# Moving every large SBUF tile of a hybrid decoder layer to an address that is a multiple of 256 bytes

## The chip, the cores and the metric

One core of a Trainium2 chip runs the whole program in one launch. The metric is the device time of one execution in microseconds; the median of three runs before the change is 1642.38 us (1641.95 to 1642.83).

## The reference, cut to what matters

One decoder layer on 1024 tokens of width 1024, all in float32. Everything that the change can touch is matrix products and the tiles that feed them:

```
n    = rmsnorm(x)
p    = n @ w_in                     # columns: z 1024 | x 1024 | B 256 | C 256 | dt 16 | q, k, v 1024 each
dt   = softplus(p_dt + dt_bias)     # 16 heads
y_s  = SSD(conv(x, B, C), dt) * silu(z), grouped rmsnorm
y_a  = (softmax(q1 k1) - lambda softmax(q2 k2)) v, 8 heads, causal, rmsnorm
h    = x + concat(y_s, y_a) @ w_out
h    = h + (silu(n2 @ w_gate) * (n2 @ w_up)) @ w_down,   n2 = rmsnorm(h)
out  = rmsnorm(h)
```

## The kernel before

**Products.** Both operands of a large product are split into two float32r parts, high and low (`split`, L170: a cast on ACT, then a subtraction on DVE), and `mm3` (L126) adds three matmuls in PSUM: high by high (L127), high by low (L128), low by high (L129). Each matmul has its own load of 128x128 stationary weights (PEld) and streams the other operand, the moving one: 256 or 512 columns, 264 in the pass that the change rewrites. TensorE therefore sees one weight load for each matmul all through the kernel. Transposes and the attention's `o` product are plain float32.

**Stages, in order of time.** Norm and transpose of the input (to about 48 us), the gate of group 0 with dt (`gate_dt`, two passes of 264 columns, to 75 us), convolutions and SSD scan of both groups with the second gate between them (to about 395 us, mixed with the first attention head's projections), attention (to about 865 us), the output projection (`po_s`, `po_a`, `po_b`, to about 975 us), the FFN's gate and up by seven products (`x`, `y`, `z`, to 1414 us), the down projection in the same way (`dx`, `dy`, `dz`, to the end). Outside the FFN's first part the order on each engine comes from a scheduler that simulates the program when it is built, with due times and priorities; inside `tc.manual_schedule` the order on PE is that of the code.

**SBUF.** Tiles live in pools that are laid out one behind the other; a tag with `bufs=n` owns n slots, each as large as the tag's largest tile. The addresses of this program, in bytes within a partition:

| pool | holds | first address | modulo 256 |
|---|---|---|---|
| const | ident (512), mhalf (32), pcol (276, takes 288) | 16512 | 128 |
| small | columns of 4 to 32 bytes | 17344 | 192 |
| big | nhi, nlo, yh, yl, n2, gd: 4 x 16384 | 18144 | 224 |
| wp | raw 2, wh 3, wl 3 slots of 4224 | 83680 | 224, 96, 224, 96, ... |
| a4, p4, hx, ob, cv | 4096 or 2048 a slot | 117472 and on | 224 throughout |

The slot of 4224 bytes comes from the gate pass: 4 x 264 columns x 4 bytes. It is 16.5 x 256, so neighbouring slots of `wp` differ by 128 modulo 256. `wh` has its slots at 92128, 96352 and 100576 (224, 96, 224 modulo 256), `wl` at 104800, 109024 and 113248 (96, 224, 96); all other large tiles stand at 224. In the FFN one slot holds the high and the low part of one product's weights (stationary), and the products take wh and wl slots in turn; in `proj_nat`, `out_block` and `proj_z0` a wh and a wl slot are the moving operand; in `proj_T` they are stationary; in the down projection both operands are in such slots.

**The gate pass.** `z0_raw` (L180) loads two units of 4 row blocks x 264 columns for each of two passes: pass 0 holds 16 dt columns and 248 gate columns, pass 1 the remaining 264. The raw tag has 2 slots. Pass 0 is loaded between the third and the fourth input block on SP's queue, its splits stand behind the third normalised block, and `proj_z0` (L258) runs 8 blocks of 128 tokens over 8 row blocks, 24 matmuls each, 192 in a pass. Each block's gate columns go through SiLU on ACT (L368) and to DRAM `z_d` from POOL's queue (L370).

Of the kernel before, what the change touches and what calls it, by code (L numbers as in the profile page):

```python
# [9 lines left out]
F32 = mybir.dt.float32  # L10
F32R = mybir.dt.float32r
# [6 lines left out]
P = 128  # L18
# [6 lines left out]
def tile_hybrid_block(  # L25
# [56 lines left out]
    nc.vector.memset(mhalf, -0.5)  # L82
    pcol = const.tile([P, 69], F32, name="pcol")
    CW, CB, SN, SL = 0, 48, 60, 68
# [9 lines left out]
    def norm_rows(parts, wbc, outs, name, pool=(), junk=None):  # L94
        """outs = RMSNorm of the row whose column pieces are parts; pieces in pool are weighted on Pool and scaled on ACT"""
        n, w = len(parts), DM // len(parts)
        ss = small.tile([P, n], F32, tag="ss1", name="ss_" + name)
        for i, p in enumerate(parts):
            nc.scalar.activation(outs[i] if junk is None else junk, p, AF.Square, accum_out=ss[:, i:i + 1])
        if n > 1:  # L100
            s1 = small.tile([P, 1], F32, tag="ss1", name="st_" + name)
            nc.vector.tensor_tensor(s1, ss[:, 0:1], ss[:, 1:2], op=ALU.add)
            ss = s1
        r = rstd_of(ss, DM, name)
        for i, (p, o) in enumerate(zip(parts, outs)):
            wi = wbc[:, i * w:i * w + w]
            if i in pool:
                nc.gpsimd.tensor_tensor(o, p, wi, op=ALU.mult)
                nc.scalar.mul(o, o, r)
            else:  # L110
                nc.vector.scalar_tensor_tensor(o, p, r, wi, op0=ALU.mult, op1=ALU.mult)
# [51 lines left out]

# [1 line left out]
    def load_raw(src, shape, name):  # L165
# [12 lines left out]
    w_in_k = w_in2.rearrange("(k p) c -> p k c", p=P)  # L178

    def z0_raw(a, u):  # L180
        """columns of dt and of the gate of group 0: 264 of 528"""
        raw = wp.tile([P, 4, 264], F32, tag="raw", bufs=2, name=f"wr_z0_{a}_{u}")
        k = slice(4 * u, 4 * u + 4)
        if a == 0:
            nc.sync.dma_start(raw[:, :, 0:16], w_in_k[:, k, C_DT:C_DT + 16])
            nc.sync.dma_start(raw[:, :, 16:264], w_in_k[:, k, C_Z:C_Z + 248])
        else:
            nc.sync.dma_start(raw, w_in_k[:, k, C_Z + 248:C_Z + 512])
        return raw

    def z0_unit(raw, a, u):
        hi = wp.tile([P, 4, 264], F32R, tag="wh", bufs=3, name=f"wh_z0_{a}_{u}")
        lo = wp.tile([P, 4, 264], F32R, tag="wl", bufs=3, name=f"wl_z0_{a}_{u}")
        split(hi, lo, raw)
        return hi, lo

# [1 line left out]
    xs = []  # L198
    mixw = P4([P, DM], F32, "mixw")
    for t in range(NT):  # L200
        xt = A4([P, DM], F32, f"x_{t}")
        nc.sync.dma_start(xt, x2[t * P:(t + 1) * P, :])
        xs.append(xt)
        if t == 0:
            nc.sync.dma_start(mixw, mix_norm_w[0].partition_broadcast(P))
        if t == 2:
            zraw = [z0_raw(0, u) for u in range(2)]
    nhi = [B16([P, KD, 512], f"nhi{i}") for i in range(2)]
    nlo = [B16([P, KD, 512], f"nlo{i}") for i in range(2)]
    for t in range(NT):  # L210
        norm_transpose([xs[t]], mixw, nhi, nlo, t, (CV if t % 2 else P4)([P, DM], F32, f"xm_{t}"), SC, f"n{t}",
                       (0,) if t % 2 else ())
        if t == 2:
            zus = [z0_unit(zraw[u], 0, u) for u in range(2)]

# [1 line left out]
    prow = P4([69, P], F32, "prow")  # L217
# [5 lines left out]
    nc.tensor.transpose(pps, prow, ident[:69, :69])  # L223
    nc.vector.tensor_copy(pcol, pps)
    nc.vector.tensor_scalar(pcol[:, SL:SL + 1], pcol[:, SL:SL + 1], 1.0 - LAMBDA_INIT, None, op0=ALU.mult)
# [9 lines left out]

# [1 line left out]
    def w_unit(src, shape, name, alloc=None):  # L237
# [10 lines left out]
    def proj_T(*jobs):  # L248
        """each job: a weight, a column, a name and sink(half, psum [128 columns, 512 tokens])"""
        us = [w_unit(w_k[:, :, col:col + P], [P, KD, P], name) for w_k, col, name, _ in jobs]  # L250
        for half in range(2):
            for (hi, lo), (_, _, name, sink) in zip(us, jobs):
                ps = MM([P, 512], f"mm_{name}_{half}")
                for k in range(KD):
                    mm3(ps, hi[:, k, :], lo[:, k, :], nhi[half][:, k, :], nlo[half][:, k, :], k == 0, k == KD - 1)
                sink(half, ps)

    def proj_z0(us, name, sink):  # L258
        """units of 264 columns; sink(t, psum [128 tokens, 264])"""
        for t in range(NT):  # L260
            ps = (MS if t % 4 > 1 else MM)([P, 264], f"mm_{name}_{t}")
            tk = slice((t % 4) * P, (t % 4) * P + P)
            for k in range(KD):
                hi, lo = us[k // 4]
                mm3(ps, nhi[t // 4][:, k, tk], nlo[t // 4][:, k, tk], hi[:, k % 4, :], lo[:, k % 4, :],
                    k == 0, k == KD - 1)
            sink(t, ps)

    def proj_nat(col, name, sink):
        """256 columns; sink(t, psum [128 tokens, 2 blocks from t, 256])"""  # L270
        us = [w_unit(w_in_k[:, 4 * u:4 * u + 4, col:col + 256], [P, 4, 256], f"{name}_{u}") for u in range(2)]
# [9 lines left out]

# [1 line left out]
    W16 = [P, NT, 16]  # L283
# [49 lines left out]

# [1 line left out]
    def conv_tiles(*tiles):  # L335
# [21 lines left out]
    def gate_dt():  # L357
        """the gate of group 0 and dt"""
        for a in range(2):
            zt = [None]  # L360
            w0, w = (0, 248) if a == 0 else (248, 264)

            def sink(t, ps):
                if t % 2 == 0:
                    zt[0] = CV([P, 2, w], F32, f"zt0_{a}_{t}")
                if a == 0:
                    nc.vector.tensor_tensor(adt[:, t, :], ps[:, 0:16], hv[:, 0, :], op=ALU.add)
                nc.scalar.activation(zt[0][:, t % 2, :], ps[:, 264 - w:], AF.Silu)  # L368
                if t % 2 == 1:
                    nc.gpsimd.dma_start(z_d[t - 1:t + 1, :, w0:w0 + w].rearrange("t p c -> p t c"), zt[0])  # L370
            proj_z0(zus if a == 0 else [z0_unit(z0_raw(1, u), 1, u) for u in range(2)], f"z0_{a}", sink)

# [138 lines left out]

# [1 line left out]
    cneg = sp.tile([P, P], F32, tag="cs", name="cneg")  # L513
# [13 lines left out]
    def v_pair(hh):  # L527
        # [head][block] views of the two heads; in the last pair but one, the heads' tiles are freed one by one
        by_head = hh == NH // 2 - 2
# [129 lines left out]

# [1 line left out]
    KG = 4  # L661
# [14 lines left out]
    def out_block(t, kys, ws, name, bank=MM):  # L676
        """two token blocks from t, 256 columns"""
        ps = bank([P, 2, 256], f"po_{name}_{t}")
# [47 lines left out]

# [1 line left out]
    # gate and up by Winograd's seven products: A are two column tiles by two halves of the contraction, B the two  # L728
    # halves of the contraction by two halves of the tokens; C = A B is summed up in PSUM (X, Y and Z)
    ORDER = (1, 2, 6, 5, 7, 3, 4)  # L730
# [4 lines left out]
    def room(p, early):  # L735
        """an operand B: [hi or lo][block of 128 rows] views of 512 tokens"""
        if early:
# [59 lines left out]
    def ffn_pair(pr, raws, order=ALL, ybank=SC):  # L797
        """silu(gate) * up of two column tiles; they and their sums as operands of the down projection to g_d"""
        sg, tm, c22, reg, sm = {}, {}, {}, [{}, {}], [{}, {}]
# [145 lines left out]
    def final_half(t, nh, last):  # L945
        """the first half of a row to be ready is weighted before its scale is known"""
        ho = h_parts(ho_all, t)
# [12 lines left out]

    # down, by the same seven products: A are the two halves of the tokens by two row tiles, B the row tiles by two
    # halves of the columns
    SLOT = {2: 0, 4: 1, 1: 2, 7: 3, 5: 4, 6: 5, 3: 6}
# [28 lines left out]
    for gi, prs in enumerate(groups):  # L992
# [5 lines left out]
        def psums(two, name):  # L998
            """four banks: one for each block of 128 tokens of a half"""
            if two:  # L1000
# [81 lines left out]
```

## Time and profile before

| | |
|---|---|
| median of 3 runs | 1642.38 us |
| the profiled execution, first to last instruction | 1643.3 us (no other time of it is recorded; 0.9 us above the median) |
| TensorE clock granted, mean | 0.995 |
| PE, weight loads, DVE, ACT, POOL busy | 97%, 84%, 65%, 47%, 26% of the span |
| DMA | 172.78 MB, mean 105 GB/s |

A matmul's record lasts longer than its share of TensorE, since matmuls overlap: 512 columns have a record of about 0.39 us and the next one starts after about 0.23 us. What a matmul costs is the distance from its start to the start of the next, and that is read from the timeline: the first and the last start of a stretch, divided by the matmuls between them. Where a row of the timeline merges n instructions, their spacing is (length - one record) / (n - 1).

### The profile page before, as it was taken

The numbers are of one execution on the slowest core, as the hardware profiler recorded it, in microseconds if no ns is written. First come the engines' busy times: TensorE is split into PE (matmuls) and PEld (weight loads), VectorE is DVE, ScalarE is ACT, GpSimd is POOL, SyncE is SP. The second block draws the span as 40 slices with busy tenths as digits, with TensorE's granted clock in tenths as the row PEclk, the third lists the DMA queues.
The fourth block names the chain that finished last, engine by engine and source line by source line (L and its number), as shares of the span: only waits on it lengthen the run. The fifth ranks groups of instructions, "written<-read, shape, count | busy, mean of one in ns | idle before, by whom it ended". The sixth has DMA issues, their size and how long they took to land. (4 is left out here: it accounts for less than half of the span.)

```text
span 1643.3 us, 23716 instructions
## 1 busy us (share of the span) xinstructions
PE 1597.2 (97%) x9170; PEld 1386.9 (84%) x9170; DVE 1071.6 (65%) x1682; ACT 775.8 (47%) x1608; POOL 429.2 (26%) x378
## 2 busy tenths in 40 slices
PE   6999999999999999999999998999999999999997
PEld 6988878887989989889999987888888888778885
DVE  5345745688776676677674477455555555898987
ACT  6444764456555565575552245333333333334445
POOL 4100330032000000013300034444444443542322
PEclk9999999999999999999999999999999999999999
DMA  5321451143011110147523221233333323944122
GB/s 195 110 79 52 129 163 56 36 142 92 24 46 39 46 33 27 45 130 229 162 77 116 84 99 56 96 102 104 111 116 118 98 96 134 365 166 186 39 103 103
DMA packets 105291, 172.78 MB, mean 105 GB/s; under 512 B 7813, under 2 KB 75530, under 8 KB 103770
## 3 DMA queue, kind: packets, MB, share of 16 engines
q1 hardware_dynamic: 95210, 137.11, 25.2%
q0 software_dynamic: 9968, 34.15, 6.3%
q8 instruction: 72, 1.18, 0.3%
q14 instruction: 41, 0.34, 0.1%
HBM read 125.82 MB, written 45.42 MB: 104 GB/s over the span
## 5 line engine op out<-in xcount | busy, mean ns | idle before, releaser
L127 PE MATMUL x<-n,wa 128*128 128x512 f32 x352 | 138.7, 396 | 0.0
L128 PE MATMUL x<-n,wa 128*128 128x512 f32 x352 | 138.7, 394 | 0.0
L129 PE MATMUL x<-n,wa 128*128 128x512 f32 x352 | 137.8, 394 | 0.0
L590 ACT ACTIVATE p<-s,nmx 128x256 f32<-128x256 f32 (+7 forms) x128 | 94.4, 740 | 53.2 <-DVE nmx L588 49.9
L172 ACT CAST wa<-s 128x512 fp32r<-128x512 f32 x88 | 54.7, 622 | 132.3 <-PE x L129 59.4
L173 DVE TENSOR_TENSOR wa<-s,wa 128x512 fp32r<-128x512 f32 x88 | 76.8, 873 | 51.1 <-ACT wa L172 50.8
L172 ACT CAST dg<-gd 128x512 fp32r<-128x512 f32 x77 | 47.7, 620 | 114.7 <-PE dx L129 57.2
L588 DVE TENSOR_REDUCE nmx<-s 128x1 f32<-128x256 f32 (+7 forms) x128 | 95.3, 754 | 2.4
L173 DVE TENSOR_TENSOR dg<-gd,dg 128x512 fp32r<-128x512 f32 x77 | 66.2, 862 | 23.3 <-ACT dg L172 23.2
L129 PEld LDWEIGHTS x<-n,wa 128*128 128x128 f32 x352 | 66.5, 189 | 15.1
L128 PEld LDWEIGHTS x<-n,wa 128*128 128x128 f32 x352 | 66.6, 189 | 14.8
L127 PEld LDWEIGHTS x<-n,wa 128*128 128x128 f32 x352 | 66.6, 189 | 14.8
L127 PE MATMUL mm_z<-wh_z,nhi 128*128 128x264 f32 (+1 forms) x256 | 75.9, 298 | 2.3 <-ACT wh_z L172 2.3
L611 PE MATMUL o<-v,p 128*128 128x128 f32 x576 | 77.7, 275 | 0.0
L129 PE MATMUL mm_z<-wh_z,nlo 128*128 128x264 f32 (+1 forms) x256 | 77.3, 303 | 0.0
L611 PEld LDWEIGHTS o<-v,p 128*128 128x128 f32 x576 | 73.5, 191 | 2.7
L128 PE MATMUL mm_z<-wl_z,nhi 128*128 128x264 f32 (+1 forms) x256 | 75.0, 294 | 0.0
L127 PE MATMUL mm_v<-wh_v,nhi 128*128 128x256 f32 x256 | 74.2, 290 | 0.0
L129 PE MATMUL mm_v<-wh_v,nlo 128*128 128x256 f32 x256 | 74.1, 290 | 0.0
L128 PE MATMUL mm_v<-wl_v,nhi 128*128 128x256 f32 x256 | 73.5, 287 | 0.0
L128 PE MATMUL po_a<-wl_wo,yh 128*128 128x256 f32 x256 | 72.6, 283 | 0.0
L91 POOL TENSOR_TENSOR rs_o<-ms_o,mhalf 128x4 f32<-128x4 f32 x16 | 18.0, 1125 | 208.4 <-DVE ms_o L89 208.3
(331 smaller groups left out, 5172.9 us busy)
## 6 DMA issues: line engine op xcount, KB each, us to landing
gd<-g_d SPq DMA_DIRECT2D x11, 1792.0 KB, 7.8
wr_g<-in_w_gate_dram SPq DMA_DIRECT2D x22, 512.0 KB, 3.8
wr_u<-in_w_up_dram SPq DMA_DIRECT2D x22, 512.0 KB, 4.3
g_d<-sg SPq DMA_DIRECT2D x22, 512.0 KB, 5.1
wr_d<-in_w_down_dram SPq DMA_DIRECT2D x22, 512.0 KB, 5.0
L<-cs_d POOLq DMA_DIRECT2D x16, 512.0 KB, 4.4
wr_y<-yT_d SPq DMA_DIRECT2D x16, 512.0 KB, 3.8
wr_wo<-in_w_out_dram SPq DMA_DIRECT2D x16, 512.0 KB, 3.5
```

The source lines that it names most:

```text
L91: nc.gpsimd.tensor_tensor(r, ms, mhalf[:, :w], op=ALU.pow)
L127: nc.tensor.matmul(ps, lh, rh, start=first, stop=False, skip_group_check=more)
L128: nc.tensor.matmul(ps, lh, rl, start=False, stop=False, skip_group_check=more)
L129: nc.tensor.matmul(ps, ll, rh, start=False, stop=last, skip_group_check=more)
L172: nc.scalar.copy(hi, raw)
L173: nc.vector.tensor_tensor(lo, raw, hi.bitcast(F32), op=ALU.subtract)
L588: nc.vector.reduce_max(nmx[:, m:m + 1], s[:, :Lk], axis=AX.X, negate=True)
L590: nc.scalar.activation(p[:, :Lk], s[:, :Lk], AF.Exp, bias=nmx[:, m:m + 1], accum_out=sm[:, m:m + 1])
L611: nc.tensor.matmul(o, wT[:, j * P:(j + 1) * P], vt[h % 2][j], start=(j == 0), stop=(j == i))
```

## The change

`pcol` grows from 69 to 77 columns (276 to 308 bytes; in blocks of 32 that is 288 to 320), which moves everything behind it by 32 bytes, so 18144 becomes 18176 = 71 x 256. The gate pass is cut anew: pass 0 has 272 columns (16 of dt, 256 of the gate) in three units of 3, 3 and 2 row blocks, pass 1 has 256 columns in two units of 4. The largest unit is then 4096 bytes, the eight slots of `wp` take 4096 bytes each, and with that every slot of big, wp, a4, p4, hx, ob and cv stands at a multiple of 256. Comments and docstrings are dropped too. Cut to its core:

```
-    pcol = const.tile([P, 69], F32, name="pcol")
+    pcol = const.tile([P, 77], F32, name="pcol")
...
+    Z0 = ((272, (0, 3, 6, 8)), (256, (0, 4, 8)))
+
     def z0_raw(a, u):
-        raw = wp.tile([P, 4, 264], F32, tag="raw", bufs=2, name=f"wr_z0_{a}_{u}")
-        k = slice(4 * u, 4 * u + 4)
+        w, ks = Z0[a]
+        k = slice(ks[u], ks[u + 1])
+        raw = wp.tile([P, ks[u + 1] - ks[u], w], F32, tag="raw", bufs=2, name=f"wr_z0_{a}_{u}")
         if a == 0:
             nc.sync.dma_start(raw[:, :, 0:16], w_in_k[:, k, C_DT:C_DT + 16])
-            nc.sync.dma_start(raw[:, :, 16:264], w_in_k[:, k, C_Z:C_Z + 248])
-        else:
-            nc.sync.dma_start(raw, w_in_k[:, k, C_Z + 248:C_Z + 512])
+        nc.sync.dma_start(raw[:, :, w - 256:], w_in_k[:, k, C_Z + a * 256:C_Z + a * 256 + 256])
         return raw
 
     def z0_unit(raw, a, u):
-        hi = wp.tile([P, 4, 264], F32R, tag="wh", bufs=3, name=f"wh_z0_{a}_{u}")
-        lo = wp.tile([P, 4, 264], F32R, tag="wl", bufs=3, name=f"wl_z0_{a}_{u}")
+        w, ks = Z0[a]
+        shape = [P, ks[u + 1] - ks[u], w]
+        hi = wp.tile(shape, F32R, tag="wh", bufs=3, name=f"wh_z0_{a}_{u}")
+        lo = wp.tile(shape, F32R, tag="wl", bufs=3, name=f"wl_z0_{a}_{u}")
         split(hi, lo, raw)
-        return hi, lo
+        return [(hi[:, k, :], lo[:, k, :]) for k in range(shape[1])]
...
-            zraw = [z0_raw(0, u) for u in range(2)]
+            zraw = [z0_raw(0, u) for u in range(3)]
...
-            zus = [z0_unit(zraw[u], 0, u) for u in range(2)]
+            zus = [z0_unit(zraw[u], 0, u) for u in range(3)]
...
-    def proj_z0(us, name, sink):
+    def proj_z0(us, w, name, sink):
+        ks = [k for u in us for k in u]
         for t in range(NT):
-            ps = (MS if t % 4 > 1 else MM)([P, 264], f"mm_{name}_{t}")
+            ps = (MS if t % 4 > 1 else MM)([P, w], f"mm_{name}_{t}")
             tk = slice((t % 4) * P, (t % 4) * P + P)
-            for k in range(KD):
-                hi, lo = us[k // 4]
-                mm3(ps, nhi[t // 4][:, k, tk], nlo[t // 4][:, k, tk], hi[:, k % 4, :], lo[:, k % 4, :],
-                    k == 0, k == KD - 1)
+            for k, (hi, lo) in enumerate(ks):
+                mm3(ps, nhi[t // 4][:, k, tk], nlo[t // 4][:, k, tk], hi, lo, k == 0, k == KD - 1)
             sink(t, ps)
...
-            w0, w = (0, 248) if a == 0 else (248, 264)
+            w = Z0[a][0]
...
-                    zt[0] = CV([P, 2, w], F32, f"zt0_{a}_{t}")
+                    zt[0] = CV([P, 2, 256], F32, f"zt0_{a}_{t}")
...
-                nc.scalar.activation(zt[0][:, t % 2, :], ps[:, 264 - w:], AF.Silu)
+                nc.scalar.activation(zt[0][:, t % 2, :], ps[:, w - 256:], AF.Silu)
```

More of the change, by code (lines that the diff above doesn't have):

```diff
@@ L223, in tile_hybrid_block @@
     nc.tensor.transpose(pps, prow, ident[:69, :69])
-    nc.vector.tensor_copy(pcol, pps)
+    nc.vector.tensor_copy(pcol[:, :69], pps)
     nc.vector.tensor_scalar(pcol[:, SL:SL + 1], pcol[:, SL:SL + 1], 1.0 - LAMBDA_INIT, None, op0=ALU.mult)
@@ L360, in gate_dt @@
             zt = [None]
-            w0, w = (0, 248) if a == 0 else (248, 264)
+            w = Z0[a][0]
             def sink(t, ps):
                 if t % 2 == 0:
-                    zt[0] = CV([P, 2, w], F32, f"zt0_{a}_{t}")
+                    zt[0] = CV([P, 2, 256], F32, f"zt0_{a}_{t}")
                 if a == 0:
                     nc.vector.tensor_tensor(adt[:, t, :], ps[:, 0:16], hv[:, 0, :], op=ALU.add)
-                nc.scalar.activation(zt[0][:, t % 2, :], ps[:, 264 - w:], AF.Silu)
+                nc.scalar.activation(zt[0][:, t % 2, :], ps[:, w - 256:], AF.Silu)
                 if t % 2 == 1:
-                    nc.gpsimd.dma_start(z_d[t - 1:t + 1, :, w0:w0 + w].rearrange("t p c -> p t c"), zt[0])
-            proj_z0(zus if a == 0 else [z0_unit(z0_raw(1, u), 1, u) for u in range(2)], f"z0_{a}", sink)
+                    nc.gpsimd.dma_start(z_d[t - 1:t + 1, :, a * 256:a * 256 + 256].rearrange("t p c -> p t c"), zt[0])
+            proj_z0(zus if a == 0 else [z0_unit(z0_raw(1, u), 1, u) for u in range(2)], w, f"z0_{a}", sink)
     def gate(g):
```

## The prediction

> **What bounds the kernel now.** I read the page first, then the busy times of eleven stretches (the table of windows), then single rows of the timeline, since the question is what one matmul costs.
>
> ```profile
> span 1643.3 us, 23716 instructions
> PE 1597.2 (97%) x9170; PEld 1386.9 (84%) x9170; DVE 1071.6 (65%) x1682; ACT 775.8 (47%) x1608; POOL 429.2 (26%) x378
> ```
> ```profile
> core 0: us, PE busy (x) PEld busy (x) DVE busy (x) ACT busy (x) POOL busy (x), PEclk, DMA share, GB/s
> 8.00:75.00 67.00, 59.91 (x450) 58.79 (x451) 32.58 (x62) 36.22 (x60) 20.99 (x19) 0.97 0.42 138
> ...
> 301.50:395.00 93.50, 91.45 (x557) 76.88 (x556) 77.87 (x123) 52.77 (x122) 21.75 (x28) 1.00 0.31 97
> 395.00:718.00 323.00, 323.00 (x2041) 290.03 (x2040) 222.64 (x436) 190.62 (x470) 17.01 (x21) 1.00 0.15 45
> ...
> 1010.00:1414.00 404.00, 404.00 (x1758) 329.92 (x1756) 210.26 (x263) 135.07 (x225) 179.43 (x124) 1.00 0.34 114
> 1414.00:1634.00 220.00, 215.51 (x925) 172.48 (x923) 198.64 (x283) 97.89 (x184) 77.25 (x56) 1.00 0.38 146
> ```
> PE is busy 97% of the span at the full clock (1.00 from 75 us on). In the FFN, 1010 to 1414 us, it never stops: 404.00 us for 1758 matmuls, 229.8 ns each. DMA is at 0.42 of its engines or below in these rows. So time is matmuls times spacing, except in the down projection, where DVE is busy 198.64 of 220.00 us. I take the median as the base; the profiled span is 0.9 us above it.
>
> **What one matmul costs, by address.** These rows are from the timeline, first and last start of a stretch of back-to-back matmuls.
>
> ```profile
> 1201.05 0.39 PE L127 MATMUL y<-n,wa 128*128 128x512 f32 x1
> ...
> 1203.77 0.39 PE L127 MATMUL z<-n,wa 128*128 128x512 f32 x1
> 1204.23 0.40 PE L127 MATMUL x<-n,wa 128*128 128x512 f32 x1
> ...
> 1207.02 0.39 PE L127 MATMUL x<-n,wa 128*128 128x512 f32 x1
> 1502.80 0.39 PE L127 MATMUL dz<-dw,dg 128*128 128x512 f32 x1
> ...
> 1505.13 0.39 PE L129 MATMUL dz<-dw,dg 128*128 128x512 f32 x1
> 929.24 0.28 PE L128 MATMUL po_b<-wl_wo,yh 128*128 128x256 f32 x1
> ...
> 932.00 0.28 PE L127 MATMUL po_b<-wh_wo,yh 128*128 128x256 f32 x1
> 872.47 0.28 PE L127 MATMUL po_a<-wh_wo,yh 128*128 128x256 f32 x1
> ...
> 875.27 0.28 PE L127 MATMUL po_a<-wh_wo,yh 128*128 128x256 f32 x1
> 100.59 0.39 PE L127 MATMUL mm_x<-nhi,wh_x 128*128 128x512 f32 x1
> ...
> 102.67 0.39 PE L127 MATMUL mm_x<-nhi,wh_x 128*128 128x512 f32 x1
> 41.87 0.28 PE L127 MATMUL mm_z<-wh_z,nhi 128*128 128x264 f32 x1
> ...
> 42.97 0.28 PE L127 MATMUL mm_z<-wh_z,nhi 128*128 128x264 f32 x1
> ```
> Product `y` at 1201 has its weights in the slot at 92128 and its moving operand in a big tile, both at 224 modulo 256: 12 matmuls in 2.72 us, **226.7 ns**. Product `x` at 1204 has its weights in the slot at 96352 (96 modulo 256): 12 in 2.79 us, **232.5 ns**, same shape, same loads. `dz` has the moving operand at 96 and the stationary one at 224: 10 in 2.33 us, 233.0. With 256 columns: `po_b`, all operands at 224, 23 in 2.76 us, **120.0**; `po_a`, where wl stands at 96, 24 in 2.80 us, 116.7. `mm_x` mixes both: 9 in 2.08 us, 231.1. The gate pass: 9 in 1.10 us, 122.2.
>
> Two things follow. First, two operands that are 128 apart modulo 256 cost 5.8 ns of a 512-column matmul; the change removes that. Second, where both stand at 224, 256 more columns cost 226.7 - 120.0 = 106.7 ns, 0.4167 ns a column, so 512 columns need 213.3 ns and each matmul carries 13.3 ns on top, exactly 32 columns, and 32 columns of float32 are 128 bytes. One explanation is that SBUF is read in whole pieces of 128 bytes: a row of 2048 bytes that starts at 224 touches 17 of them instead of 16, and one of 1024 bytes 9 instead of 8. (The neighbours 224 and 96 are both 96 modulo 128, so no slot of this kernel shows an aligned start.) The nearest rows for an aligned moving operand are the transposes: they stream `ident`, at 16512 = 129 x 128.
>
> ```profile
> 105.45 1.03 PE L394 MATMUL btp<-ident,BT 128*128 128x128 f32 x8
> 834.68 1.05 PE L611 MATMUL o<-v,p 128*128 128x128 f32 x8
> L607 PE MATMUL wtp<-ident,p 128*128 128x128 f32 x288 | 46.7, 273 | 1.2 <-ACT o L613 1.2
> L611 PE MATMUL o<-v,p 128*128 128x128 f32 x576 | 77.7, 275 | 0.0
> ```
> Transposes: (1.03 - 0.273) / 7 = 108 to 109 ns; `o`, same shape, moving operand at 224: (1.05 - 0.275) / 7 = 110.7. If a plain float32 column takes two column times, 128 take 106.7, and the aligned overhead is 2.3 ns. That gives my estimate for an aligned matmul: 213.3 + 2.3 = **215.6 ns** for 512 columns, 106.7 + 2.3 = **109.0** for 256. Bounds: below, 213.3 (nothing on top); above, 233.0, the `dz` row, since nothing excludes that equal starts collide. I take the value next to the transposes.
>
> The Trainium skill ("TensorE: Matmul & The Clock Gate", section Back-to-back issue gap) gives N / 2.4 + 2.5 ns, 215.8 and 109.2, with no word on addresses; by it the sum below would be 1 us smaller.
>
> **The change part by part.** The counts follow from the loops (mm_k: 8 heads x 2 halves x 8 blocks x 3), as these groups by shape show; L128 and L129 count as L127.
>
> ```profile
> L127 PE MATMUL mm_v<-wh_v,nhi 128*128 128x256 f32 x256 | 74.2, 290 | 0.0
> L127 PE MATMUL po_a<-wh_wo,yh 128*128 128x256 f32 x256 | 72.3, 282 | 0.0
> L127 PE MATMUL po_s<-wh_wo,yh 128*128 128x256 f32 x128 | 37.1, 290 | 0.4 <-DVE QL L563 0.4
> L127 PE MATMUL mm_x<-nhi,wh_x 128*128 128x512 f32 x128 | 50.7, 396 | 0.0
> ```
> - FFN: 1758 x (229.8 - 215.6) = **-25.0 us**. DVE (210 of 404) and POOL (179) leave room, so all of it counts.
> - Down: 924 (11 pairs x 7 products x 4 x 3) x 14.2 = -13.1 us. DVE would then be busy 198.6 of 207; it is what waits next, so I take half, **-6.6**.
> - 512 columns elsewhere: 384 each of mm_x, mm_k and mm_q, 96 each of mm_B and mm_C, 192 scores, 1536 x (231.1 - 215.6) = -23.8 us.
> - 256 columns: 768 mm_v, 768 po_a, 384 each of po_s, po_b and the second gate, 2688. From between 116.7 and 120.0 I take 118, so 2688 x 9.0 = -24.2 us. Of these two only part shortens the chain: in 301 to 395 us DVE is busy 77.87 of 93.50. I take four fifths, **-38.4**.
> - Gate pass: pass 1, 192 x (122.2 - 109.0) = -2.5; pass 0, 8 columns more at 0.4167 ns, 192 x 3.3 = +0.6 (its row blocks are 1088 bytes, so they start at 0, 64, 128 or 192 modulo 256, and I count no gain). **-1.9**.
>
> Then what the three units cost.
>
> ```profile
> 2.67 0.74 SPq L185 DMA_DIRECT2D wr_z<-in_w_in_dram  x1
> 3.45 0.53 SPq L186 DMA_DIRECT2D wr_z<-in_w_in_dram  x1
> ...
> 6.59 4.41 SPq L202 DMA_DIRECT2D x<-in_x_dram  x5
> 13.89 2.42 DVE L173 TENSOR_TENSOR wl_z<-wr_z,wh_z 128x1056 fp32r<-128x1056 f32 x2
> 15.17 1.55 SPq L188 DMA_DIRECT2D wr_z<-in_w_in_dram  x2
> 16.77 1.09 SPq L218 DMA_DIRECT2D prow<-in_conv_w_dram  x1
> 51.29 1.08 ACT L172 CAST wh_z<-wr_z 128x1056 fp32r<-128x1056 f32 x1 [1.30 <-PE mm_z L129]
> 52.40 1.26 DVE L173 TENSOR_TENSOR wl_z<-wr_z,wh_z 128x1056 fp32r<-128x1056 f32 x1 [2.87 <-ACT wh_z L172]
> ```
> The third unit finds both raw slots taken until the first split ends, at about 15.1 us (half of the 2.42 us row). If SP stands still there, the five input blocks behind it, issued from 6.59 us, come up to 8.5 us late; if the scheduler issues them first, nothing. It has put L188 ahead of L218, which precedes it in the code, so I take **+0.5** (two more issues, 0.74 + 0.53, mostly hidden). ACT and DVE do one split more for the same 4224 elements; both are busy about half of this stretch, no cost. Between the passes all three wh slots are held by pass 0 where before one was free: pass 1's first split (1.08 + 1.26 us) starts after the last use of unit 0, 15 matmuls (1.8 us) before the pass ends, so PE waits up to **+0.8**. The gate's stores stay four a pass.
>
> Sum: -25.0 - 6.6 - 38.4 - 1.9 + 1.3 = -70.6, so 1642.4 - 70.6 = **1572 us**.
>
> **The rivals.**
>
> *Phase only.* The 32 columns are not a split piece but the price of the weight load, 128 weights at four a column time; then they stay, and all that goes is the difference between slots. FFN 1758 x 3.1 = -5.4, down half of 2.9, -1.4; 512 columns 1536 x 4.4 = -6.8, but 256 columns go from 118 to 120.0, +5.4, four fifths of both -1.1; gate -0.4 + 0.6, units +1.3. **1636 us.** For it: 13.3 ns at both widths fits as well. Against it: transposes load 128 weights each and show no such 32 columns. The same page of the Trainium skill (section Part 2, on LDWEIGHTS) says that "Loading the next tile's weights doesn't steal SBUF read bandwidth from the running matmul", which speaks against this rival too.
>
> *Addresses don't matter*: the 5.8 ns belong to the products' order, not to their slots, and only the units' 1.3 us and the gate pass count: **1643 us**. Against it: the same difference in FFN and down. The Trainium skill ("SBUF — State Buffer", Specifications) speaks of lines of 16 bytes, of which every start at a multiple of 32 is one; by that rule alone this rival would hold. The 226.7 and 232.5 ns, both at multiples of 32, disagree with it as it stands.
>
> *Equal starts collide* (the other side). With all tiles at 0, moving operand and weights ask for the same piece at the same moment, and each 512-column matmul takes the 233.0 ns of `dz`, 256 columns 120: +5.6 + 2.9 + 0.8 x (2.9 + 5.4) + 1.3 = +16: **1659 us**. It decides once a 512-column matmul takes more than 230 ns. Against it: both at 224 also start alike, and that is the fast row.
>
> That tiles miss the multiples is excluded by arithmetic (18176 = 71 x 256, 83712 = 327 x 256).
>
> **How the numbers follow.** Pieces 0.44, phase only 0.26, no effect 0.13, collision 0.17. The likeliest gives 1572; its own range is 1552 (DVE limits nowhere, all -88 us count) to 1600 (a third of the effect lost to waits). A range that leaves out 2 in 10 reaches over phase only and no effect, to 1645. A measurement here tells about 0.2%, 3.3 us. Faster: pieces, phase only and little else, 0.71; same 0.13; slower 0.16.
>
> **What would show it.** In the changed profile: `x`, `y` and `z` spaced 215 to 217 ns, `po_b` 109 to 110, no difference between products of neighbouring slots; FFN near 380 us; DVE at 95% or more of the down projection; the five input blocks still issued by 7 us. Spacings of 227 and 120 mean phase only. The sum fails if waits of ACT and DVE in attention grow as fast as the matmuls shrink.

## The result: 1627.3 us, 15 us faster where 70 were forecast, and the profile after

| | before | after |
|---|---|---|
| median of the runs beside each other | 1642.16 us (1641.7 to 1642.83) | 1627.34 us (1625.65 to 1628.72) |
| ratio, 95% interval | | 0.9907 (0.9893 to 0.9921) |
| profiled execution, first to last instruction | 1643.3 us | 1624.6 us |

The sign was right and the size was not: the likeliest case gave 1572 us, and the time lies inside the range (1552 to 1645) only because the range reaches over the rival *phase only* (1636 us).

First the page of the changed kernel, then its busy times by stretch (columns as before: us, then busy time and instructions of PE, PEld, DVE, ACT and POOL, then the granted clock and DMA). The stretches are shifted by the time gained up to there.

```profile
span 1624.6 us, 23724 instructions
PE 1583.5 (97%) x9170; PEld 1386.3 (85%) x9170; DVE 1075.0 (66%) x1683; ACT 775.6 (48%) x1609; POOL 431.6 (27%) x378
```
```profile
core 0: us, PE busy (x) PEld busy (x) DVE busy (x) ACT busy (x) POOL busy (x), PEclk, DMA share, GB/s
8.00:75.00 67.00, 62.09 (x463) 60.27 (x464) 34.93 (x65) 38.68 (x65) 21.77 (x20) 1.00 0.41 139
...
1000.00:1394.00 394.00, 394.00 (x1739) 326.33 (x1739) 211.85 (x262) 133.48 (x222) 176.22 (x123) 1.00 0.33 114
1400.00:1615.00 215.00, 209.20 (x910) 169.41 (x908) 193.75 (x279) 96.44 (x182) 74.96 (x54) 1.00 0.37 142
```

The shares hardly move: PE is busy 97% of a shorter span, DVE 66%. In the FFN PE still never stops (394.00 of 394.00), and 1739 matmuls in it are 226.6 ns each, against 229.8 before. That is the size of the effect here: 3.2 ns of a matmul, not 14.2. No other engine became the bound; DVE has 193.75 of 215.00 us in the down projection, 90%, where I expected 95% or more.

The timeline of the changed kernel, first and last start of stretches of back-to-back matmuls, as in the prediction:

```profile
862.28 0.28 PE L127 MATMUL po_a<-wh_wo,yh 128*128 128x256 f32 x1
...
868.04 0.28 PE L127 MATMUL po_a<-wh_wo,yh 128*128 128x256 f32 x1
...
918.08 0.28 PE L127 MATMUL po_b<-wh_wo,yh 128*128 128x256 f32 x1
...
920.84 0.28 PE L129 MATMUL po_b<-wh_wo,yl 128*128 128x256 f32 x1
...
1190.24 0.39 PE L127 MATMUL x<-n,wa 128*128 128x512 f32 x1
...
1194.54 0.39 PE L128 MATMUL x<-n,wa 128*128 128x512 f32 x1
...
1488.56 0.39 PE L129 MATMUL dz<-dw,dg 128*128 128x512 f32 x1
...
1490.38 0.39 PE L129 MATMUL dz<-dw,dg 128*128 128x512 f32 x1
```

`x`: 19 distances in 4.30 us, 226.3 ns. `dz`: 8 distances in 1.82 us, 227.5. `po_b`: 23 distances in 2.76 us, 120.0, what it took at 224 modulo 256. `po_a`: 48 distances in 5.76 us, 120.0, and it took 116.7 before. (The rows give hundredths of a microsecond, so the shorter stretches are good to about 1 ns.) So products with mixed starts (232.5, 233.0) came down to the value that equal starts already had, nothing went below it, and the 256-column products that were mixed became dearer.

### The profile page after: what moved, and what is told of

Same layout as the page of the kernel before. It is cut to its first block, busy times and chain, and to the rows that moved or that the text cites. A ratio compares the mean times of both kernels' runs of the same rounds, so it can differ in the third digit from the quotient of the medians.

```text
span 1624.6 us, 23724 instructions
## 1 busy us (share of the span) xinstructions
PE 1583.5 (97%) x9170; PEld 1386.3 (85%) x9170; DVE 1075.0 (66%) x1683; ACT 775.6 (48%) x1609; POOL 431.6 (27%) x378
## 5 line engine op out<-in xcount | busy, mean ns | idle before, releaser
L127 PE MATMUL mm_z<-wh_z,nhi 128*128 128x256 f32 (+1 forms) x256 | 75.3, 297 | 2.1 <-ACT wh_z L172 2.1
L129 PE MATMUL mm_z<-wh_z,nlo 128*128 128x256 f32 (+1 forms) x256 | 76.7, 300 | 0.0
L128 PE MATMUL mm_z<-wl_z,nhi 128*128 128x256 f32 (+1 forms) x256 | 74.9, 293 | 1.6 <-DVE wl_z L173 1.6
```

The source lines that it names most:

```text
L127: nc.tensor.matmul(ps, lh, rh, start=first, stop=False, skip_group_check=more)
L128: nc.tensor.matmul(ps, lh, rl, start=False, stop=False, skip_group_check=more)
L129: nc.tensor.matmul(ps, ll, rh, start=False, stop=last, skip_group_check=more)
```

## The experiments

Three theories were open after the result. *Phase*: only the distance between the start of the moving and of the stationary operand modulo 256 counts. *Multiple*: the multiple of 256 itself gives a part. *Cut*: the new cut of the gate pass carries the gain. And one question lay below them: what are the 13.3 ns beyond the columns, if not a split piece?

### slots224: all tiles in phase, but off the multiple

```
-    pcol = const.tile([P, 77], F32, name="pcol")
+    pcol = const.tile([P, 69], F32, name="pcol")
```

> The changed kernel with pcol back at 69 columns: every large tile stands at 224 modulo 256 instead of 0, all still in the same phase. Phase theory (only the distance between the start of the moving and of the stationary operand modulo 256 counts, the absolute start does not): as the changed kernel, 1627 us (1624 to 1630), 512 columns spaced 226.7 ns, 256 columns 120.0. Rival, the multiple of 256 itself gives part of the gain (a start at 0 saves a split piece on some reads): 1632 us or more, 512 columns above 228 ns.

Measured: 1629.44 us (1626.97 to 1633.22), ratio to the kernel before 0.9918 (0.9904 to 0.9933). The FFN of its trace:

```profile
1191.54 0.39 PE L127 MATMUL x<-n,wa 128*128 128x512 f32 x1
...
1195.62 0.39 PE L127 MATMUL x<-n,wa 128*128 128x512 f32 x1
```

18 distances in 4.08 us, 226.7 ns. From its first start to that of the down projection (964.61 to 1397.81 us) the FFN takes 433.20 us, in the changed kernel 433.19, and the interval overlaps that of the changed kernel widely. So the multiple of 256 itself adds nothing that this run can show. Whether the rest is equal starts or the cut is left to the next run.

### cut4224: the new cut alone, at the old addresses

```
-        hi = wp.tile(shape, F32R, tag="wh", bufs=3, name=f"wh_z0_{a}_{u}")
-        lo = wp.tile(shape, F32R, tag="wl", bufs=3, name=f"wl_z0_{a}_{u}")
+        hi = z0_view(wp.tile([P, 1056], F32R, tag="wh", bufs=3, name=f"wh_z0_{a}_{u}"), shape[1], w)
+        lo = z0_view(wp.tile([P, 1056], F32R, tag="wl", bufs=3, name=f"wl_z0_{a}_{u}"), shape[1], w)
```

(raw in the same way, and `pcol` of 69 columns)

> The changed kernel's gate pass (272 columns in three units, then 256 in two), but slots of 4224 bytes and pcol of 69 columns, so that all addresses are those of the kernel before (224, 96, 224, 96 modulo 256 in the weight slots). Phase theory: only what the new cut does at the start is left, -3.3 us as the two traces differ at 33 us, so 1639 us (1637 to 1642), with spacings of 231 and 118 ns. Rival, the new cut (another order from the scheduler, three shorter units) carries the gain: 1630 us or less.

Measured: 1639.14 us (1635.26 to 1643.04), 0.9976 (0.9966 to 0.9987), as the phase theory said. Its FFN (964.57 to 1404.33 us) takes 439.77 us, close to the 440.37 of the kernel before. So of 15 us the cut is about 4, and the addresses are the other 11. By these traces `mm_x` starts at 97.82 us before and at 94.71 with the new cut, 3.1 us earlier. A part of that is seen in the rows of both kernels between 22 and 29 us. Before:

```profile
24.19 2.35 POOL L108 TENSOR_TENSOR xm<-x,mixw 128x1024 f32<-128x1024 f32 x1
24.26 3.36 DVE L111 SCALAR_TENSOR_TENSOR xm<-x,rs_n,mixw 128x1024 f32<-128x1024 f32 x1 [0.80 <-POOL rs_n L91]
...
27.54 1.28 DVE L124 TENSOR_TENSOR nlo<-pt_n,nhi 128x512 fp32r<-128x512 f32 x2
...
28.27 0.66 PE L120 MATMUL pt_n<-ident,xm 128*128 128x128 f32 x4 [3.88 <-DVE nlo L124]
```

With the new cut (cut4224):

```profile
23.01 0.65 PE L120 MATMUL pt_n<-ident,xm 128*128 128x128 f32 x4 [1.29 <-DVE nlo L124]
...
23.02 1.30 DVE L111 SCALAR_TENSOR_TENSOR xm<-x,rs_n,mixw 128x1024 f32<-128x1024 f32 x1
23.22 3.34 POOL L108 TENSOR_TENSOR xm<-x,mixw 128x1024 f32<-128x1024 f32 x1
...
24.45 2.69 DVE L173 TENSOR_TENSOR wl_z<-wr_z,wh_z 128x544 fp32r<-128x544 f32 x1
...
27.19 0.39 PE L128 MATMUL mm_z<-wl_z,nhi 128*128 128x272 f32 x1 [1.43 <-DVE wl_z L173]
```

Before, DVE's `xm` starts 0.07 us after POOL's `xm` and takes 3.36 us; in cut4224 the same instruction takes 1.30. Behind the slow one stands `nlo`, for which PE's transposes wait 3.88 us. In the other order POOL's `xm`, now the second, takes 3.34 us instead of 2.35, then the short low split takes 2.69 us for 544 elements, and PE waits 1.29 + 1.43 = 2.72. The Trainium skill ("SBUF — State Buffer", Who interferes with whom) says that a DVE instruction with two SBUF inputs contends with a GpSimd instruction that reads SBUF, and that the order of issue decides who is blocked; these rows agree with it.

PE's waits up to `mm_x` sum to 15.0 us before and 13.5 with the new cut, so they explain 1.5 of the 3.1 us. The rest fits the clock. In the kernel before, TensorE ran at a granted clock of 0.50 from 29.07 to 32.48 us, beginning 0.8 us after the long wait had ended, with PE busy throughout; in the trace of cut4224 it did not:

```profile
8.00:42.00 34.00, 26.91 (x178) 25.79 (x179) 21.41 (x35) 24.10 (x41) 17.36 (x14) 0.95 0.53 178
```

The clock of 0.95 over these 34 us is 1.00 in cut4224 and in the changed kernel. By estimate 3.41 us at half the clock cost 1.7 us of full speed, and 1.5 + 1.7 make up the 3.1. That the wait brought the stretch at half the clock is not shown. Nor is the share of the clock in the 4 us between the medians: the trace of cut4224 is that of its fastest execution (1635.26 us, mean clock 0.999), and its others had 0.994 to 0.998, those of the kernel before beside them 0.993 to 0.996.

### map: what a matmul costs at each pair of starts

```
+    for a in range(8):
+        for b in range(8):
+            group("w" + L[a] + L[b], sl(mv, 32 * a, 512), sl(wt, 32 * b, P), 512)
+            ...
+    def group(name, m, w, n, count=24, rows=P):
+        for i in range(count):
+            nc.tensor.matmul(o, w, m, start=i == 0, stop=i == count - 1)
```

> Leaves out the whole layer: TensorE alone, groups of 24 matmuls of one shape, each with its own weight load, the moving operand and the stationary one at every pair of starts that are multiples of 32 modulo 256, at 512 and at 256 columns; then other widths, bfloat16, fewer stationary columns. Theory 1, the 13.3 ns are the price of the load of 128 stationary columns: 226.7 and 120.0 ns for all eight pairs of equal starts, 0 included; with 96, 64 and 32 stationary columns 223.3, 220.0 and 216.7; widths 128, 192, 320, 384 and 448 cost 66.7, 93.3, 146.7, 173.3 and 200.0. Theory 2, a fixed gap of each matmul whatever it loads: 226.7 for 96, 64 and 32 stationary columns as well. Theory 3, the 13.3 ns come from what the other engines and the DMAs do to SBUF: nothing else runs here, so 216 and 109 ns. Starts 128 apart: 233 at 512 columns by the phase theory, and 117 or less on the mean at 256.

Groups are named by width (w: 512, n: 256 columns) and by the starts of the moving and of the stationary operand (a to h: 0, 32, ... 224); bf is bfloat16 (bfo: both operands 96 bytes on), fp plain float32 (fpo: both 224 bytes on), stat_h has 64 stationary columns. In the timeline a group is one row: start, length, count.

```profile
20.49 5.61 PE L83 MATMUL waa<-mv,wt 128*128 128x512 f32 x24
...
42.74 5.76 PE L83 MATMUL wae<-mv,wt 128*128 128x512 f32 x24
...
371.45 5.61 PE L83 MATMUL whh<-mv,wt 128*128 128x512 f32 x24
376.90 3.03 PE L83 MATMUL naa<-mv,wt 128*128 128x256 f32 x24
...
597.78 5.69 PE L83 MATMUL stat_h<-mv,wt 128*64 128x512 f32 x24
...
639.10 5.34 PE L83 MATMUL bf_c<-mb,wb 128*128 128x512 bf16 x24
...
648.24 5.34 PE L83 MATMUL bfo_c<-mb,wb 128*128 128x512 bf16 x24
...
658.78 10.53 PE L83 MATMUL fp_b<-mf,wf 128*128 128x256 f32 x48
...
674.50 10.53 PE L83 MATMUL fpo_b<-mf,wf 128*128 128x256 f32 x48
```

The distance is (length - one record) / (count - 1), with records of 0.39 and 0.28 us: 227.0 for waa (both at 0) and 227.0 for whh (both at 224), 233.5 for wae; 119.6 for naa. All 128 pairs, as means over the eight groups of one distance:

| stationary start minus moving start, modulo 256 | 0 | 32 | 64 | 96 | 128 | 160 | 192 | 224 |
|---|---|---|---|---|---|---|---|---|
| 512 columns, ns | 226.8 | 233.1 | 233.4 | 233.9 | 233.4 | 233.4 | 229.2 | 233.4 |
| 256 columns, ns | 119.6 | 118.3 | 116.9 | 118.0 | 118.7 | 119.9 | 117.8 | 117.6 |

At 512 columns the eight pairs of one distance lie within 1.4 ns of each other, so only the distance counts, and distance 0 is alone at the bottom. At 256 columns distance 0 is among the dearest, but there the pairs of one distance differ by up to 3.9 ns, so the distance alone does not decide; at 128 the mean is 118.7, where 117 or less was expected. TensorE ran alone here: theory 3 (other engines, DMAs) falls. Theory 1 falls as well: with 64 stationary columns (5.69 - 0.39) / 23 = 230.4 ns, and not 220. And a fixed gap (theory 2) falls by bfloat16: (5.34 - 0.38) / 23 = 215.7 ns at either start. There is the value that I had forecast for float32r, and it comes without any change of address. (Both operands were moved together; unequal starts were not tried in bfloat16 or plain float32.) Plain float32 shows it too: (10.53 - 0.38) / 47 = 216.0 ns for each of two records of a 256-column matmul, 0.84 ns a column, and the same 10.53 us with both operands at 224 (fpo_b).

### map2: the moving operand or the stationary one

```
+        same("mzw", mv[:, 0:1].to_broadcast([P, 512]), sl(wt, 0, P), 512)
+        same("bsw", mb.rearrange("p (n two) -> p two n", two=2)[:, 0, 0:512], wb[:, 0:P], 512)
+        same("bws", mb[:, 0:512], wb.rearrange("p (n two) -> p two n", two=2)[:, 0, 0:P], 512)
+        group("pn" + L[a] + L[b], [(h, s0), (l, s0), (h, s1)] * 16, 256)
```

> Leaves out the whole layer, as map does, whose groups showed bfloat16 at 215.8 ns for 512 columns at 0 and at 96 alike, float32r at 226.7 for equal starts, and no fall at 512 columns with fewer stationary columns (96, 64, 32: 230, 230, 232), while 256 columns fell from 119.3 to 116.0, 113.7 and 113.3. Theory S, what is paid is the reading of the moving operand at 4 bytes a column: a moving operand that is one element again and again costs 216 and 109 ns, bfloat16 read with every second element (4 bytes a column too) rises above 216, and with 32 stationary columns the extra grows with the width. Theory L, what is paid is the reading of the stationary operand: the one element costs 226.7 and 120 as before, bfloat16 with every second element in the stationary operand rises, in the moving one it does not, and the extra falls with the stationary columns at every width. Orders of the kernel's own three matmuls: with 256 columns moving, all eight starts for high by eight for low, I expect about 120 for equal starts (0, 0) and 116 to 118 for most others; with 512 columns the weights stationary, 226.7 at (0, 0), nothing below it, and 231 to 233 for most.

```profile
20.82 5.92 PE L86 MATMUL pnaa<-mv,wt 128*128 128x256 f32 x48
...
32.33 5.82 PE L86 MATMUL pnac<-mv,wt 128*128 128x256 f32 x48
...
779.78 2.89 PE L86 MATMUL stn_e<-mv,wt 128*64 128x256 f32 x24
...
874.39 4.32 PE L86 MATMUL wd_l<-mv,wt 128*32 128x384 f32 x24
...
922.84 5.41 PE L86 MATMUL mzw<-mv,wt 128*128 128x512 f32 x24
...
930.78 5.59 PE L86 MATMUL bsw<-mb,wb 128*128 128x512 bf16 x24
...
938.93 5.34 PE L86 MATMUL bws<-mb,wb 128*128 128x512 bf16 x24
```

One element of float32r read 512 times (mzw): (5.41 - 0.38) / 23 = 218.7 ns, 8 less than a row of 512. bfloat16 with every second element as the moving operand, 4 bytes a column (bsw): 226.1, 10 more than dense bfloat16. The same step in the stationary operand (bws): 215.7, nothing. So at 512 columns most of what is paid is the reading of the moving operand at 4 bytes a column: theory S, which had 216 for the single element and so leaves 3 ns unexplained. At 256 columns the single element came to 112.0 (109 expected). S is not all: with 64 stationary columns 256 columns cost 113.5 (stn_e) where 128 cost 120, so there the stationary operand has a part of some 6 ns. That part does not follow the number of its columns: 112 stationary columns cost 113.3 and 48 cost 118.0. And S's growth with the width did not show clearly: with 32 stationary columns the extra was about 13 at 320, 352 and 384 columns (wd_l: (4.32 - 0.34) / 23 = 173.0), 15 at 416, 16 at 448, 13 at 480 and 18 at 512.

Of the kernel's own order with 256 columns, high and low both at 0 (pnaa) cost (5.92 - 0.28) / 47 = 120.0 and low at 64 (pnac) 117.9. With 512 columns (0, 0) was the cheapest of 64 pairs, 228.7, if only just: the others took 228.9 to 235.2.

### opposite, wl64, and the changed kernel beside them

opposite puts 128 bytes before the weight slots (and 128 behind them):

```
+    off = ctx.enter_context(tc.tile_pool(name="off", bufs=1))
+    nc.vector.memset(off.tile([P, 32], F32, name="off"), 0.0)
     wp = ctx.enter_context(tc.tile_pool(name="wp", bufs=1))
```

> The changed kernel with the eight weight slots 128 bytes further on (128 modulo 256), everything else at 0. Phase theory, with the prices of map and map2 (512 columns 227 in phase, 233 for starts 128 apart; 256 columns 120 in phase, 118.7): FFN +1758 x 6 = +10.5, the transposed projections +1344 x 5.5 = +7, 256 columns 2688 x -1.2 = -3, down 0 (both of its operands lie in such slots): +14, about 1642 us, FFN longer by 10 us. Rival, the gain came from the even spacing of the slots (all alike, whatever their phase) or from the cut: no change, 1627 us.

wl64 starts the low part of 256 columns 64 bytes into its slot:

```
+        tl = wp.tile([P, 1088], F32R, tag="wl", bufs=3, name=name)
+        return tl[:, 16:16 + shape[1] * 256].rearrange("p (k c) -> p k c", c=256)
```

> The changed kernel, but the low part of a unit of 256 columns starts 64 bytes into its slot (slots of 4352 bytes); products of 512 columns keep equal starts. map2 gives 117.8 ns for this order (high at 0, low at 64) against 120.0 for (0, 0): about 2300 matmuls of 256 columns have their low part in such a slot, 2300 x -1.9 = -4.4 us, 1623 us, 0.997 of the changed kernel. Rival, that in the kernel the waits between stages take the gain of the 256-column products, as they did in the attention: 1626 to 1628 us though mm_v and po_a are spaced 118.

> The changed kernel itself once more, beside the next two on one chip: 0.990 to 0.992 of the kernel before, 1627 to 1630 us.

| kernel | us | ratio to the kernel before |
|---|---|---|
| after_again | 1628.52 (1625.48 to 1631.33) | 0.9911 (0.9897 to 0.9924) |
| opposite | 1639.22 (1635.91 to 1640.8) | 0.9978 (0.9968 to 0.9988) |
| wl64 | 1626.78 (1624.96 to 1627.78) | 0.9903 (0.9889 to 0.9916) |

The first start of the FFN and the first of the down projection, in after_again and then in opposite:

```profile
967.55 0.48 PE L127 MATMUL x<-n,wa 128*128 128x512 f32 x1
...
1400.74 0.62 PE L127 MATMUL dx<-dw,dg 128*128 128x512 f32 x2
```
```profile
963.74 0.47 PE L127 MATMUL x<-n,wa 128*128 128x512 f32 x1
...
1195.52 0.39 PE L127 MATMUL x<-n,wa 128*128 128x512 f32 x1
...
1200.86 0.40 PE L129 MATMUL x<-n,wa 128*128 128x512 f32 x1
...
1406.99 0.62 PE L127 MATMUL dx<-dw,dg 128*128 128x512 f32 x2
```

The FFN takes 433.19 us in after_again and 443.25 in opposite, +10.1 for +10.5 expected; `x` is spaced 5.34 us / 23 = 232.2 ns. All slots are alike in opposite, they hold 4096 bytes, and the cut is the new one: only the distance to the big tiles differs, and it takes back 10.7 of the 14 us that lie between after_again and the kernel before on this chip. opposite and cut4224 end at the same time, 1639 us. The whole came out 3 us below the +14 expected. The down projection, both of whose operands lie in the moved slots, did not get longer (227.2 us, 227.7 in after_again). Over all runs the FFN takes 433.2 us in the four traces with equal starts (after, after_again, slots224, wl64), and 440.4, 439.8 and 443.3 in the three without (the kernel before, cut4224, opposite). The traces of cut4224 and opposite have no stretch at half the clock in the FFN and the others 3.4 to 6.8 us of it, so the clock does not make this difference.

wl64 is 1.7 us below after_again, which these intervals can't tell from nothing; -4.4 was expected. Its trace says why:

```profile
861.90 0.28 PE L127 MATMUL po_a<-wh_wo,yh 128*128 128x256 f32 x1
...
866.10 0.28 PE L129 MATMUL po_a<-wh_wo,yl 128*128 128x256 f32 x1
```

35 distances in 4.20 us, 120.0 ns: in this stretch the steady 120 came back all the same, though the low parts stand at 64. Over all steps of `po_a` without a pause the mean is 119.4 (119.8 in after_again), over those of `mm_v` 118.4 (119.2). The 117.8 of map2 carried over by less than half, so the rival given with the expectation, waits between stages, was hardly put to the test.

## Why the prediction was wrong, step by step

The stages by their first starts: `mm_x` and the FFN of the kernel before and of the changed one.

```profile
97.82 0.39 PE L127 MATMUL mm_x<-nhi,wh_x 128*128 128x512 f32 x1
973.62 0.49 PE L127 MATMUL x<-n,wa 128*128 128x512 f32 x1
1413.99 0.62 PE L127 MATMUL dx<-dw,dg 128*128 128x512 f32 x2
```
```profile
94.54 0.39 PE L127 MATMUL mm_x<-nhi,wh_x 128*128 128x512 f32 x1
963.31 0.48 PE L127 MATMUL x<-n,wa 128*128 128x512 f32 x1
1396.50 0.62 PE L127 MATMUL dx<-dw,dg 128*128 128x512 f32 x2
```

| term of the sum | forecast | the traces show |
|---|---|---|
| FFN | -25.0 | 440.37 to 433.19 us: -7.2 |
| down | -6.6 | 229.3 to 228.1 us: -1.2 |
| 512 and 256 columns elsewhere | -38.4 | 875.80 to 868.77 us: -7.0 (872.84 us and -3.0 by after_again) |
| gate pass and units | -1.9 + 1.3 | 97.82 to 94.54 us: -3.3 |
| sum | -70.6 | -18.7 between these two executions, -14.8 between the medians |

Not all of the -18.7 is the price of matmuls. PE's idle time fell by 5.0 us (span less busy time on the two pages: 46.1 before, 41.1 after). Between 20 us and the last matmuls the trace before has three stretches of 3.41 us at a granted clock of 0.50, from 29.1, 223.6 and 991.6 us, and that of the changed kernel one, from 981.5; PE was busy in them, so the two that are missing are worth about 3.4 us by estimate. (after_again, the same kernel, has two, from 23.0 and 985.6 us, so such a stretch comes and goes between executions.) What is left, some 10 us, is spacing. The means over all steps without a pause in the two traces give as much (FFN -6.6, down -2.8, the other 512 columns -4.6, the 256 columns +3.5), and opposite took back 10.7. The prediction had put the clock at nothing ("1.00 from 75 us on"); its own table of windows has 0.99 from 165 to 301.5 us and 0.98 from 920.5 to 1010.

**The step that failed** is "32 columns of float32 are 128 bytes", the reading of the 13.3 ns as a split piece, and with it the aligned values 215.6 and 109.0 on which every large term rests. The 13.3 ns stand at 0 as at 224 (waa and whh, 227.0 both). My arithmetic of 13.3 ns at both widths was right, and it fitted two mechanisms; I gave more weight to the one that the change would remove. At 512 columns most of the extra belongs to the reading of a moving operand at 4 bytes a column (bsw against dense bfloat16, mzw against a full row).

**The inference that misled me** was the transposes. They show 108 to 109 ns, I took this for the effect of the address 129 x 128, and `o` at 224 with 110.7 for the proof of the contrary. But they are plain float32, which spends about two column times on each column of a record (fp_b, 216.0 ns for 256); so it does not read 4 bytes in each column time, and it shows the same price at 0 and at 224 (fp_b and fpo_b). A row of another type was no row for the aligned price. The bound above (233.0) and the row of equal starts (226.7) were the only rows of the same kind, and both were measured; the value that I took lay outside everything that the trace showed of this kind of matmul.

**What held.** The 5.8 ns between mixed and equal starts, read from `y` and `x`, were right and were removed, in FFN and down. *Phase only* gave 227 and 120.0 ns, and these came. Its 1636 us did not: most of the 9 us by which the kernel came below it lie at the start (-3.3 us for +1.5), in idle time and in the clock, and it was silent on the last two. Its argument for the 32 columns, the price of the weight load, failed at 512 columns: fewer stationary columns left them at 230. So the rival's spacings were right and its reason half wrong. The Trainium skill ("TensorE: Matmul & The Clock Gate", Part 2) says that loading the next weights takes no read bandwidth from the running matmul. Taken as no contention at all it doesn't fit: at 256 columns the time falls from 120 to 113.5 when 64 instead of 128 columns are loaded, and the start of the stationary operand alone moves 512 columns by 6 ns. Its gap of N / 2.4 + 2.5 for an isolated matmul (the same page of the Trainium skill, Back-to-back issue gap) agrees with the spacing of bfloat16, 215.7 for 215.8, and not with that of float32r, 227.0.

*Collision* is refuted (equal starts are the cheapest at 512 columns), *no effect* by opposite.

**The 256-column terms** had the wrong sign: the means over all steps without a pause went from 118 or 119 to between 119 and 120 (`po_a` 117.9 to 119.8, `mm_v` 118.3 to 119.2) instead of 109; over 2688 matmuls that is +3.5 us and not -24. The 512-column term gave -4.6 and not -23.8. `mm_x` fell from 231.6 to 226.9, but `mm_k` and `mm_q` only to 230; the 192 scores, whose tiles stood at equal starts before as well, were counted in the term and gained nothing. The FFN's term also took the 1758 matmuls of its window for the whole, which has 1848; that is 1.3 us by the forecast price.

**The units** were forecast at +1.3 and gave about -4 (cut4224). One piece of that step was right: the scheduler issued the third unit behind the five input blocks, which went out from 6.12 us on, and not ahead of them. The wait between the passes (+0.8) hardly came: PE is idle for 0.2 us between 42 and 75 us. What I had not foreseen is that the new order moves DVE's `xm` out from under POOL's, and that the clock at the start could differ.

**What stays open.** Why distance 0 is the cheapest at 512 columns and among the dearest at 256, and why the extra is 13.3 ns for several widths, no run here explains, nor why `mm_k` and `mm_q` stop at 230. The stage between `mm_x` and the FFN differs by 4.1 us between two executions of the same changed kernel (868.77 and 872.84). That is nearly all PE's waiting, which sums to 7.7 us in the first and 11.3 in the second at the same clock; what makes the waits differ is open.

## What to carry to other kernels

Before a fixed part of a time is put down to one cause, find a row of the same type at the other end of that cause, or treat both ends as open: a row of plain float32 said nothing about float32r. With float32r products whose every matmul loads its weights, place the stationary and the moving operand of 512-column products at the same start modulo 256; the absolute start does not matter. For 256 columns it is one to three ns the other way, and what a loop of one pattern shows need not hold in the kernel.

## What the runs showed of the hardware

- The cost of a 512-column float32r matmul follows the distance of the two starts modulo 256: 226.8 ns at 0, 229.2 at 192, 233.1 to 233.9 at the other six multiples of 32. No start by itself mattered: equal starts cost 226.7 to 228.0 ns at all eight.
- 4 bytes a column in the moving operand cost 8 to 10 ns of 512 columns in both types tried: bfloat16 215.7 dense, 226.1 with every second element; float32r 227.0, and 218.7 from a single element.
- Below 256 columns float32r gains little, since the load of 128 weights sets the pace. In map2 192 columns came no faster than 111.7 ns (from 839.82 to the next group at 842.50, 24 matmuls); with 32 stationary columns they took (2.28 - 0.25) / 23 = 88.3:

```profile
837.70 2.28 PE L86 MATMUL wd_f<-mv,wt 128*32 128x192 f32 x24
839.82 2.84 PE L86 MATMUL we_f<-mv,wt 128*128 128x192 f32 x24
842.50 2.64 PE L86 MATMUL wd_g<-mv,wt 128*32 128x224 f32 x24
```
- A stretch of narrow matmuls (64 to 128 columns) ran at half the clock in the same run, though PE's records fill it without a gap:

```profile
812.00:830.00 18.00, 18.00 (x113) 18.00 (x113) 0.67 (x5) 0.00 (x0) 0.00 (x0) 0.50 0.00 1
```
